# Two products of the next chunk placed ahead of the first output part, and a later load of each chunk's second weight block

## The chip, the core and the metric

The kernel runs on one core of a Trainium2 chip. The metric is the time of one execution on the device in microseconds (us), and the figure for a kernel is the median of several executions. A profiled execution is recorded separately; its trace gives a start and a duration for every instruction of the engines TensorE (PE), VectorE (DVE), ScalarE (ACT) and GpSimd (POOL), and for the transfers that SyncE (SP) issues.

## What is computed

The reference is a two-layer backbone over 512 latent tokens and 256 context tokens of width 1024. Each layer is a SwiGLU half-step, a mixer (a short gated convolution in layer 0, attention in layer 1) and a second SwiGLU half-step. Only the SwiGLU matters here:

```python
def norm_modulate(x, g, shift, scale):
    return rms_norm(x, g) * (1 + scale) + shift

def swiglu(h, w_in, w_out):
    gate, up = jnp.split(h @ w_in, 2, axis=-1)
    return (jax.nn.silu(gate) * up) @ w_out

h = norm_modulate(x_lat, norm_g[i, 0], m_lat[:, 0, 0], m_lat[:, 0, 1])
x_lat = x_lat + MACARON_WEIGHT * m_lat[:, 0, 2] * swiglu(h, ffn_w_in[i, 0], ffn_w_out[i, 0])
```

`w_in` has 2 x 2816 columns and `w_out` 2816 rows. Latent and context tokens share the weights, so a sub-layer works on 768 tokens (512 in the last one).

## The kernel before

**Precision.** Every fp32 weight block is split into a high part (ACT, line 186) and a low part (DVE, line 187), and so is every activation. A product is three matmuls: high by high, high by low, low by high (lines 818 to 820).

**Chunks.** The 2816 columns are 22 chunks of 128 gate and 128 up columns. A chunk c has two raw weight blocks of 512 KB: (c, 0), the gate, and (c, 1), the up columns. Each of the two holds two halves of the contraction, so a chunk has four quarters, `quad(0)` to `quad(3)`. The first few chunks of a sub-layer ("direct" ones: three in the first sub-layer, two in the other SwiGLU ones) are computed by plain products. All later ones use a seven-product scheme over the two halves of the tokens and of the contraction: M1 to M7, with weights that are a quarter or a sum of quarters. M1 and M2 use `quad(0)` and `quad(1)`, which both lie in block (c, 0). M5 is the first that needs block (c, 1): line 354 subtracts a quarter of it, line 363 adds one, and lines 186 and 187 split the result. Below, M1(3) is product M1 of chunk 3.

**Banks of PSUM.** The first sub-layer has three banks A, three C, one B and one S. M1 of a chunk opens a bank A that M6, M7 and M4 go on using; M2 takes the one bank B, which DVE empties at line 1086; M5 opens a bank C for M3. The bank of M1 is copied by ACT at line 1084.

**Output parts.** After chunks 0 and 1 comes output part 0: for each of eight blocks m of `w_out`, a product for the 512 latent tokens and one for the 256 context tokens, each in its own bank. `out_banks` takes the banks C and A in turn. DVE adds each bank, times the gate, to x at line 886. The first three blocks are interleaved, so three banks fill together.

**Order.** PE and SP run in the order in which the code is written; `product_order` gives it, in the first sub-layer with `boot=True`:

- twelve steps of the direct chunks (positions 0 to 11), then M1(3), M2(3), output part 0, M5(3), M6(3),
- then, for each chunk c from 4: M1(c), M2(c), M7(c-1), M5(c), M6(c), M4(c-1), M3(c-1).

ACT and DVE keep the written order up to the second position after the direct steps (13). Behind that a scheduler has fixed their order at build time; it may also put a later instruction in front of an earlier one. At run time each engine works through its own list in order, and a wait holds up all that stands behind it. `hooks` carry other work of the sub-layer by position: the normed activations, their sums T1 to T4, and the splits of these (lines 736 to 778).

**Weights in flight.** Raw blocks go through five buffers (`RAWS`), loaded by SP at line 216 in the order of the list `raws`; a load waits until a buffer is given back, which for the four `w_out` blocks of part 0 (256 KB each) is when both of their splits are done, and for a chunk's two blocks when M3 is prepared. Split weights go through eight buffers (`GRANULES`).

Of the kernel before, what the change touches and what calls it, by code (L numbers as in the profile page):

```python
# [85 lines left out]
def product_order(count, parts, direct, boot=False):  # L86

    ends = {}
    at = 0
    for pi, n in enumerate(parts):
        at += n
        ends[at - 1] = pi
    order = []

    def done(c):  # L100
        if c in ends:
            order.append((ends[c], "out"))

    if boot:
        order += [(c, half + k) for half, k in ("00", "01", "10") for c in range(direct)]
        order += [(c, "11") for c in reversed(range(direct))]
    else:
        order += [(c, h + k) for h in "01" for c in range(2) for k in "01"]
        for c in range(2, direct):
            order += [(c, "10"), (c, "00"), (c, "11"), (c, "01")]  # L110
    order += [(direct, m) for m in ("M1", "M2")]
    for c in range(direct):
        done(c)
    order += [(direct, m) for m in ("M5", "M6")]
    for c in range(direct + 1, count):
        order += [(c, "M1"), (c, "M2"), (c - 1, "M7"), (c, "M5"), (c, "M6"), (c - 1, "M4")]
        if c == count - 1:
            order.append((c, "M7"))
        order.append((c - 1, "M3"))
        done(c - 1)  # L120
    order += [(count - 1, "M4"), (count - 1, "M3")]
    done(count - 1)
    return order
# [3 lines left out]
def backbone(ctx: ExitStack, tc: tile.TileContext, a: dict, out: bass.AP):  # L127
# [23 lines left out]
    def ptile(name, shape=(P, 512)):  # L151
        pool, tag = bank[name]
        return pool.tile(list(shape), F32, name=f"ps_{name}", tag=tag)
# [31 lines left out]
    def split(dsth, dstl, src):  # L185
        act.activation(dsth, src, AF.Copy)  # L186
        dve.tensor_tensor(out=dstl, in0=src, in1=dsth.bitcast(F32), op=ALU.subtract)  # L187
# [6 lines left out]
    raw_tiles = {}  # L194

    def raw_add(src, shape, users):
        raws.append((src, shape, users))
        return len(raws) - 1
# [25 lines left out]
    def raw_used(n):  # L224
        raw_tiles[n][1] -= 1
        if not raw_tiles[n][1]:
            raw_tiles.pop(n)
            if n not in raw_homes:
                raw_state["open"] -= 1
# [64 lines left out]
    def add_plain(raw, u, ks, where=None, event=None):  # L294
        def make(dh, dl):
            split(dh, dl, raw_tiles[raw][0][:, u, ks])
            raw_used(raw)
        stream.append((event, where, ks.stop - ks.start, make))
# [9 lines left out]
    def add_out(w, k0, npart, held=None, key="", events=(None, None), extra=None, event=None):  # L308
        for m in range(0, KC, 2):
            n = raw_add(w[:, m : m + 2, k0 : k0 + npart, :], (2, npart), 2)  # L310
            for u in range(2):
                mm = m + u
                if held and mm // 3 < len(held):
                    add_plain(n, u, slice(0, npart), (key, held[mm // 3], mm % 3), events[mm // 3])
                else:
                    where = extra() if extra else None
                    add_plain(n, u, slice(0, npart), where, event if where else None)

    def add_products(key, sources, order, parts, direct, out_w, held, home=lambda c, kh: None, between=None):

        raw = {}
        seen = set()

        def need(c, which):
            if (c, which) not in raw:
                raw[c, which] = raw_add(sources[c][which], (1, KC), 2 if c < direct else 1)

        for c, which in ((0, 0), (0, 1), (1, 0), (1, 1)):
            need(c, which)
        for c, m in order:  # L330
            if m == "out":
                last = c == len(parts) - 1
                outs = out_w(c)
                add_out(*outs, held=held if last else None, key=f"{key}held", events=((key, "M5"), (key, "M6"), (key, "M3")))
                continue
            for which in range(2):
                need(c, which)
            if (c, m) == (0, "10") and between:
                between()
            if c >= direct:  # L340
                add_product(raw[c, 0], raw[c, 1], m)
            elif (c, m[1]) not in seen:
                seen.add((c, m[1]))
                k0 = 4 * int(m[1])
                for which in range(2):
                    where = home(c, int(m[1]))
                    add_plain(raw[c, which], 0, slice(k0, k0 + 4), where and ("home", (*where, which)))

    def add_product(g, u, m):
        def quad(q):  # L350
            return raw_tiles[g if q < 2 else u][0][:, 0, slice(4 * (q % 2), 4 * (q % 2) + 4)]

        def sub(o, x, y):
            dve.tensor_tensor(out=quad(o), in0=quad(x), in1=quad(y), op=ALU.subtract)  # L354

        def make(dh, dl):
            if m == "M1":
                split(dh, dl, quad(0))
            elif m == "M2":
                split(dh, dl, quad(1))  # L360
            elif m == "M5":
                sub(0, 0, 2)
                dve.tensor_tensor(out=quad(2), in0=quad(2), in1=quad(3), op=ALU.add)
                split(dh, dl, quad(2))
            elif m == "M6":
                sub(2, 3, 0)
                split(dh, dl, quad(2))
            elif m == "M7":
                split(dh, dl, quad(0))
            elif m == "M4":  # L370
                split(dh, dl, quad(3))
            else:
                sub(1, 1, 2)
                split(dh, dl, quad(1))
                raw_used(g)
                raw_used(u)

        stream.append((None, None, 4, make))

    ffn_order = {boot: product_order(FC, FFN_PARTS, BOOT_DIRECT if boot else FFN_DIRECT, boot) for boot in (False, True)}  # L380
    conv_order = product_order(12, (6, 6), CONV_DIRECT)
    conv_pairs = []
    for j in range(0, KC, 2):
# [97 lines left out]
    ada_chunks, ada_loaded, ahead = [], {}, {}  # L481
# [69 lines left out]
    def bg():  # L551

        pace["n"] += 1
        if pace["n"] == pace["first"] - 2:
            for n in range(ahead["depth"]):
                ada_next(ahead["start"] + n)
        bg_run(1)
# [145 lines left out]
    def free_order():  # L703
        region.pop().close()
# [126 lines left out]
            got += [t[:, 0, :], t[:, 1, :]][: count - c]  # L831
        return got

    out_turn = [0]

    def out_banks(grp, count):

        got = []
        for _ in range(count):
            got.append(ptile("CA"[out_turn[0] % 2]))  # L840
            out_turn[0] += 1
        return got

# [169 lines left out]
    def out_phase(*args):  # L1013
        for _ in out_steps(*args):
            pass
# [15 lines left out]
    def products(gp, key, order, parts, direct, chunk, straight, out_args, after, passes, hooks, hold):  # L1031
# [73 lines left out]
        for n, (c, m) in enumerate(order):  # L1105
            if m == "out":
                last = c == len(parts) - 1
                if last and isinstance(after, dict):
                    out_close(*out_args(c), after)
                elif last and after == "end":  # L1110
                    out_last(*out_args(c), gp)
                else:
                    out_phase(geo.groups, passes, *out_args(c), after if last else None, out_banks, 3)
                    if n in hooks:
                        hooks[n]()
                    for go in behind_outs:
                        go()
                    behind_outs.clear()
            elif c < direct:
                directly(n, c, m)  # L1120
            else:
                product(c, m)
                bg()
            if n in hooks and m != "out":
                hooks[n]()
            if n == (steps[-1] + 2 if key == "f00" else steps[-1]):
                free_order()
# [489 lines left out]
    with tc.tile_pool(name="apool", bufs=1) as apool, tc.tile_pool(name="g0", bufs=1) as gp, tc.tile_pool(name="qp", bufs=1) as qp, psum(A=3, B=1, C=3, S=1):  # L1617
# [24 lines left out]
        with tc.tile_pool(name="boot", bufs=1) as bp, aw_pool():  # L1642
# [37 lines left out]
            def do(*items):  # L1680
                def go():
                    for name, *args in items:
                        own[name](*args) if name in own else op[name](*args)
                return go

            def scale_put():
# [19 lines left out]
                     (8, 2): do(("gate1", 1)), (8, 3): do(("gate1", 1)), (9, 0): do(("gate1", 1), ("raws",)), (9, 1): do(("gate1", 1)),  # L1706
                     (10, 0): do(("sum_parted", "T1", 0), ("sum_parted", "T1", 1), ("sums", "T2", 0), ("sums", "T2", 1)),
                     11: do(("fill", 1)), 12: do(("sums", "T3", 0), ("sums", "T3", 1)), 13: do(("sum_parted", "T2", 0), ("sum_parted", "T2", 1)),
                     14: do(("sums", "T4", 0), ("sums", "T4", 1), ("sum_parted", "T3", 0), ("sum_parted", "T3", 1), ("sum_parted", "T4", 0), ("sum_parted", "T4", 1))}
            op1 = opening(0, 1)  # L1710
            ffn(gp, 0, 0, op1, TOKENS, hooks, op)
        op2 = opening(0, 2)
# [91 lines left out]
```

## Time and profile before

| | us |
|---|---|
| median of three runs | 2451.38 |
| lowest and highest of the runs | 2450.44, 2451.80 |
| profiled execution, its own time | 2457.93 |
| span of the profiled execution (first to last instruction) | 2456.2 |
| PE busy in it | 2402.6 |
| DVE busy | 2019.5 |
| ACT busy | 1167.3 |
| mean granted PE clock | 0.993 |

The busy time of an engine says how much of the span it had work on it. PE's is nearly all of the span, so the places of interest are the few in which PE stood still, and what it waited for there. A timeline row gives start, duration, engine, line, what is written and read, the shape, how many instructions are merged, and in brackets the idle time ahead of it with what ended that. Rows overlap a little: a row's duration includes its pipeline, and the next one may start before it is over.

### The profile page before, as it was taken

The page shows a single profiled execution, that of the slowest core. Times are in us where ns is not written, and L with a number is a line of the kernel's source. Part 1 is how long each engine was busy: PE and PEld are TensorE (multiplying, and loading weights), DVE is VectorE, ACT ScalarE, POOL GpSimd, SP SyncE. Part 2 cuts the span into 40 slices and gives each one's busy share as a digit, 9 for nine tenths or more (in the row PEclk, how much of TensorE's full clock was granted, in tenths as well). Part 3 has the DMA queues.
Part 4 walks back from the last instruction along what each step waited for, and adds up shares of the span by engine and source line. Part 5 has one row for each costly group of instructions (what it writes and reads, how often), then busy time and mean ns, then how long its engine had stood idle before and what let it go on. Part 6 is the DMA issues. An engine that isn't in the chain of part 4 may idle for free.

```text
span 2456.2 us, 37712 instructions
## 1 busy us (share of the span) xinstructions
PE 2402.6 (98%) x14303; PEld 2268.6 (92%) x14303; DVE 2019.5 (82%) x4011; ACT 1167.3 (48%) x2205; POOL 134.6 (5%) x256
## 2 busy tenths in 40 slices
PE   8999999999999999999999999999999999999998
PEld 5799999999999999999999999999997889899997
DVE  5889999678988889897667999976568887887776
ACT  5544343355535643433435544344346776555545
POOL 0001111000000001110000012200000000000000
PEclk9999999999999999999999999999999999999999
DMA  8234453230333024433222146542231101133332
GB/s 310 86 121 131 144 163 121 78 121 26 95 108 126 23 75 142 159 120 104 86 66 69 51 140 209 176 130 63 68 120 53 51 1 48 57 108 101 102 104 78
DMA packets 93062, 253.71 MB, mean 103 GB/s; under 512 B 10320, under 2 KB 18640, under 8 KB 92880
## 3 DMA queue, kind: packets, MB, share of 16 engines
q1 hardware_dynamic: 71984, 183.65, 23.3%
q0 software_dynamic: 20352, 67.12, 9.2%
q8 instruction: 112, 1.84, 0.3%
q14 instruction: 70, 0.57, 0.1%
q10 hardware_dynamic: 544, 0.52, 0.1%
HBM read 249.16 MB, written 2.10 MB: 102 GB/s over the span
## 4 chain that ended last, share of the span: by engine, by line
PE 65%; issue 20%; DVE 9%; ACT 3%; DMA 3%; POOL 0%; SPq 0%; DVEq 0%; ACTq 0%; POOLq 0%
PE ps_A L818 11%; PE ps_A L819 11%; PE ps_A L820 11%; PE ps_C L818 7%; PE ps_C L819 7%; PE ps_C L820 7%; PE ps_B L818 2%; PE ps_B L819 2%; PE ps_B L820 2%; DVE w L187 2%; DVE ps_S L511 1%; DMA aw<-in_ada_t 1%; PE ps_T L1474 1%; DMA raw<-in_ffn_w_in 1%; DMA silu_row<-in_crow 1%
## 5 line engine op out<-in xcount | busy, mean ns | idle before, releaser
L186 ACT ACTIVATE w<-raw 128x512 fp32r<-128x512 f32 (+1 forms) x868 | 525.0, 619 | 705.7 <-PE ps_A L820 339.3
L187 DVE TENSOR_TENSOR w<-raw,w 128x512 fp32r<-128x512 f32 (+1 forms) x868 | 578.8, 679 | 109.1 <-ACT w L186 99.8
L818 PE MATMUL ps_C<-gh,w 128*128 128x512 f32 (+1 forms) x544 | 195.2, 359 | 12.2 <-DVE g L1100 9.1
L819 PE MATMUL ps_C<-gl,w 128*128 128x512 f32 (+1 forms) x544 | 194.1, 357 | 0.0
L820 PE MATMUL ps_C<-gh,w 128*128 128x512 f32 (+1 forms) x544 | 193.6, 356 | 0.0
L354 DVE TENSOR_TENSOR raw<-raw,raw 128x512 f32<-128x512 f32 x264 | 181.3, 689 | 12.5 <-DMA raw<-in_ffn_w_in 9.1
L489 POOL DMA_DIRECT2D aw<-in_ada_t x240 | 129.0, 538 | 1060.6 <-DVE mods L511 603.0
L818 PE MATMUL ps_A<-gh,w 128*128 128x256 f32 (+1 forms) x544 | 181.0, 333 | 3.0 <-DVE x L886 3.0
L820 PE MATMUL ps_A<-gh,w 128*128 128x256 f32 (+1 forms) x544 | 181.0, 333 | 0.0
L819 PE MATMUL ps_A<-gl,w 128*128 128x256 f32 (+1 forms) x544 | 181.0, 333 | 0.0
L511 DVE CUSTOM_DVE_ANT_0 ps_S<-aw,silu_row,mods 128x512 f32<-128x512 f32 x208 | 157.5, 757 | 11.1 <-ACT silu_row L495 9.3
L511 DVE CUSTOM_DVE_ANT_0 ps_S<-aw,silu_row,packed 128x512 f32<-128x512 f32 x208 | 157.2, 756 | 6.3 <-DMA aw<-in_ada_t 4.7
L886 DVE SCALAR_TENSOR_TENSOR x<-ps_C,gat,x 128x512 f32<-128x512 f32 (+1 forms) x156 | 102.8, 659 | 68.3 <-PE ps_C L820 68.3
L886 DVE SCALAR_TENSOR_TENSOR x<-ps_A,gat,x 128x512 f32<-128x512 f32 (+1 forms) x164 | 100.3, 611 | 41.3 <-PE ps_A L820 41.1
L818 PE MATMUL ps_A<-tB11h,w 128*128 128x384 f32 (+1 forms) x400 | 130.7, 327 | 0.2 <-ACT tB11h L758 0.2
L818 PEld LDWEIGHTS ps_C<-gh,w 128*128 128x128 f32 x544 | 103.3, 190 | 29.6 <-issue 9.1
L819 PE MATMUL ps_A<-tB11l,w 128*128 128x384 f32 (+1 forms) x400 | 130.4, 326 | 0.2 <-DVE tB11l L759 0.2
L820 PE MATMUL ps_A<-tB11h,w 128*128 128x384 f32 (+1 forms) x400 | 130.4, 326 | 0.0
L819 PE MATMUL ps_C<-tB22l,w 128*128 128x384 f32 (+2 forms) x384 | 125.2, 326 | 0.0
L820 PE MATMUL ps_C<-tB22h,w 128*128 128x384 f32 (+2 forms) x384 | 124.7, 325 | 0.0
L818 PE MATMUL ps_C<-tB22h,w 128*128 128x384 f32 (+2 forms) x384 | 124.6, 325 | 0.0
L820 PEld LDWEIGHTS ps_C<-gh,w 128*128 128x128 f32 x544 | 103.4, 190 | 15.1
(437 smaller groups left out, 6942.9 us busy)
## 6 DMA issues: line engine op xcount, KB each, us to landing
raw<-in_ffn_w_in SPq DMA_DIRECT2D x170, 512.0 KB, 4.1
aw<-in_ada_t POOLq DMA_DIRECT2D x240, 256.0 KB, 3.1
raw<-in_ffn_w_out SPq DMA_DIRECT2D x80, 512.0 KB, 4.4
raw<-in_conv_w_in SPq DMA_DIRECT2D x24, 512.0 KB, 3.7
ada<-in_ada_w SPq DMA_DIRECT2D x28, 256.0 KB, 5.3
raw<-in_attn_w_qkv SPq DMA_DIRECT2D x12, 512.0 KB, 5.0
raw<-in_ada_w SPq DMA_DIRECT2D x8, 512.0 KB, 6.7
silu_row<-in_crow POOLq DMA_DIRECT2D x8, 512.0 KB, 4.2
```

The source lines that it names most:

```text
L186: act.activation(dsth, src, AF.Copy)
L187: dve.tensor_tensor(out=dstl, in0=src, in1=dsth.bitcast(F32), op=ALU.subtract)
L354: dve.tensor_tensor(out=quad(o), in0=quad(x), in1=quad(y), op=ALU.subtract)
L489: nc.gpsimd.dma_start(w, a["ada_t"][t, kh, j])
L511: ins = dve.tensor_tensor_reduce(out=junk, in0=w, in1=silu_row[kh][:, v, :], scale=1.0, scalar=total if kh else ada_b[:, i, hm // 2, col : ...
L818: pe.matmul(ps, wh, xh, start=first, stop=False, **kw)
L819: pe.matmul(ps, wh, xl, start=False, stop=False, **kw)
L820: pe.matmul(ps, wl, xh, start=False, stop=last, **kw)
L886: dve.scalar_tensor_tensor(out=x, in0=p[:, o - off : o - off + w], scalar=gat[:, m, v : v + 1], in1=x, op0=ALU.mult, op1=ALU.add)
L1474: pe.transpose(pt[:, c, :], pr[:, (c0 + c) * P : (c0 + c + 1) * P], ident)
```

## The change

- In the first sub-layer alone (`ahead = 2`), M1(4) and M2(4) stand in front of output part 0, behind M2(3). From M7(3) on the order is what it was.
- In every sub-layer, M1 and M2 of a chunk ask for the first raw block alone; the second one is asked for at M5. This changes the order of the loads where output part 0 stands between M2 and M5: the four `w_out` blocks are then loaded ahead of the second block. That is so in all four SwiGLU sub-layers; in the first one the block (4, 0) moves ahead too.
- In the first sub-layer's part 0 the banks are taken in the turn C, B, C, A, C instead of C, A; M1(3) and M1(4) hold two of the three banks A meanwhile.
- The hook at position 14 is at 16, which is the same place behind output part 0.

```diff
-    order += [(direct, m) for m in ("M1", "M2")]
+    ahead = 2 if boot else 1
+    order += [(direct + c, m) for c in range(ahead) for m in ("M1", "M2")]
     for c in range(direct):
         done(c)
     order += [(direct, m) for m in ("M5", "M6")]
     for c in range(direct + 1, count):
-        order += [(c, "M1"), (c, "M2"), (c - 1, "M7"), (c, "M5"), (c, "M6"), (c - 1, "M4")]
+        if c >= direct + ahead:
+            order += [(c, "M1"), (c, "M2")]
+        order += [(c - 1, "M7"), (c, "M5"), (c, "M6"), (c - 1, "M4")]
...
-            for which in range(2):
+            for which in range(1 if m in ("M1", "M2") else 2):
                 need(c, which)
...
-    out_turn = [0]
+    out_turn, out_tags = [0], ["CA"]
...
-            got.append(ptile("CA"[out_turn[0] % 2]))
+            got.append(ptile(out_tags[0][out_turn[0] % len(out_tags[0])]))
...
+                    out_tags[0] = "CBCAC" if key == "f00" and c == 0 else "CA"
                     out_phase(geo.groups, passes, *out_args(c), after if last else None, out_banks, 3)
+                    out_tags[0] = "CA"
...
-                     14: do(("sums", "T4", 0), ...
+                     16: do(("sums", "T4", 0), ...
```

`add_product` gets the table of raw blocks instead of two of its numbers, so that the second block's number need not be known at M1.

More of the change, by code (lines that the diff above doesn't have):

```diff
@@ L340, in add_products @@
             if c >= direct:
-                add_product(raw[c, 0], raw[c, 1], m)
+                add_product(raw, c, m)
             elif (c, m[1]) not in seen:
@@ L347, in add_products, with add_product @@
                     add_plain(raw[c, which], 0, slice(k0, k0 + 4), where and ("home", (*where, which)))
-    def add_product(g, u, m):
+    def add_product(raw, c, m):
         def quad(q):
-            return raw_tiles[g if q < 2 else u][0][:, 0, slice(4 * (q % 2), 4 * (q % 2) + 4)]
+            return raw_tiles[raw[c, q // 2]][0][:, 0, slice(4 * (q % 2), 4 * (q % 2) + 4)]
         def sub(o, x, y):
@@ L374, in make @@
                 split(dh, dl, quad(1))
-                raw_used(g)
-                raw_used(u)
+                raw_used(raw[c, 0])
+                raw_used(raw[c, 1])
         stream.append((None, None, 4, make))
@@ L1708, in backbone @@
                      11: do(("fill", 1)), 12: do(("sums", "T3", 0), ("sums", "T3", 1)), 13: do(("sum_parted", "T2", 0), ("sum_parted", "T2", 1)),
-                     14: do(("sums", "T4", 0), ("sums", "T4", 1), ("sum_parted", "T3", 0), ("sum_parted", "T3", 1), ("sum_parted", "T4", 0), ("sum_parted", "T4", 1))}
+                     16: do(("sums", "T4", 0), ("sums", "T4", 1), ("sum_parted", "T3", 0), ("sum_parted", "T3", 1), ("sum_parted", "T4", 0), ("sum_parted", "T4", 1))}
             op1 = opening(0, 1)
```

## The prediction

> **What bounds the kernel now.** I read the busy times first, then the list of what PE waited for, and then the timelines of PE and DVE around output part 0 of the first sub-layer, where the change sits.
>
> ```profile
> PE 2402.6 (98%) x14303; PEld 2268.6 (92%) x14303; DVE 2019.5 (82%) x4011; ACT 1167.3 (48%) x2205; POOL 134.6 (5%) x256
> ```
>
> PE is busy for 98% of the span, so an edit that leaves PE's own work alone can only win back time in which PE stands still or runs on a slow clock. The list of PE's waits names two of the longest, and the timeline of PE puts both in output part 0:
>
> ```profile
> PE ps_A L818 <- DVE x L886: 3.7, 2, 3.0
> PE ps_C L818 <- ACT w L186: 2.8, 1, 2.8
> ...
> 93.47 0.34 PE L820 MATMUL ps_B<-tB21h,w 128*128 128x384 f32 x1
> 96.57 0.50 PE L818 MATMUL ps_C<-gh,w 128*128 128x512 f32 x1 [2.77 <-ACT w L186]
> 105.52 0.58 PE L818 MATMUL ps_A<-gh,w 128*128 128x256 f32 x1 [2.98 <-DVE x L886]
> 118.34 0.34 PE L818 MATMUL ps_C<-tT1h,w 128*128 128x384 f32 x1
> 122.50 0.33 PE L818 MATMUL ps_A<-tB11h,w 128*128 128x384 f32 x1
> 126.71 0.34 PE L818 MATMUL ps_A<-tT3h,w 128*128 128x384 f32 x1
> ```
>
> M2(3) ends near 93.8. PE waits 2.77 for the first split of an output weight, starts part 0 at 96.57, and stops again for 2.98 because DVE has not yet emptied a bank. M5(3) and M6(3) run from 118.34 to 122.50 (4.16 for both), M1(4) and M2(4) from 122.50 to 126.71 (4.21), where M7(3) begins. The clock by stretches, PE alone (length, PE busy with its count, granted clock, and two columns on DMA):
>
> ```profile
> 95.29:98.71 3.42, 2.14 (x9) 1.00 0.07 7
> ...
> 102.12:105.53 3.41, 0.43 (x5) 1.00 0.72 249
> 105.53:108.94 3.41, 3.41 (x11) 0.50 0.01 4
> 2139.87:2143.28 3.41, 1.41 (x13) 1.00 0.74 209
> 2143.28:2146.69 3.41, 3.41 (x19) 0.50 0.24 99
> ```
>
> After the second wait the clock is at half for 3.41 us, which costs half of that, 1.71. It fell just so after a stretch with 2.00 us idle (3.41 less 1.41).
>
> How long part 0 takes without a wait is shown by the same part in the third sub-layer, which has the same shapes:
>
> ```profile
> 857.54 0.39 PE L818 MATMUL ps_C<-gh,w 128*128 128x512 f32 x1
> 863.08 0.28 PE L818 MATMUL ps_A<-gh,w 128*128 128x256 f32 x1
> 874.24 0.34 PE L818 MATMUL ps_C<-tT1h,w 128*128 128x384 f32 x1
> ```
>
> That is 16.70 us. So from 93.8 to 126.71, 32.9 us, PE's work is 16.70 + 4.16 + 4.21 = 25.1, and 7.8 is lost: 2.77 and 2.98 of waiting, 1.71 by the half clock, and some 0.4 of slower restarts. 7.8 is 0.32% of the time, and all that the change can win here.
>
> **The first wait: does it go?** PE would now find M1(4) at 93.8 in place of part 0. What it needs is a split weight, and ACT has none ready:
>
> ```profile
> 95.69 0.52 ACT L1184 ACTIVATE gh<-gd 128x384 fp32r<-128x384 f32 x1 [0.71 <-DVE gd L1205]
> 96.12 1.94 ACT L186 ACTIVATE w<-raw 128x256 fp32r<-128x256 f32 x6
> 119.38 0.62 ACT L186 ACTIVATE w<-raw 128x512 fp32r<-128x512 f32 x1
> ```
>
> The six splits of output weights begin at 96.12, behind the last step of the direct chunks (line 1184). In the changed kernel's instruction order the two splits for M1(4) and M2(4) stand at that same place, behind line 1184 and ahead of the output weights. Could line 1184 come earlier? The change takes two operations off DVE before it:
>
> ```profile
> 80.08 0.69 DVE L354 TENSOR_TENSOR raw<-raw,raw 128x512 f32<-128x512 f32 x1
> 80.81 0.69 DVE L363 TENSOR_TENSOR raw<-raw 128x512 f32<-128x512 f32 x1
> 80.88 0.62 ACT L1173 ACTIVATE gd<-gd,bias 128x384 f32<-128x384 f32 x1 [3.40 <-DVE bias L1171]
> 81.69 0.62 DVE L1175 SCALAR_TENSOR_TENSOR gd<-gd,bias 128x384 f32<-128x384 f32 x1
> ```
>
> These are the subtraction and addition for M5(3). But the next step, line 1175, needs ACT's line 1173, which ends at 81.50. So the two hide behind that wait, their removal gains nothing, and the chain up to 96.12 stays. A split of 512 columns takes 0.62, so M1(4) starts at about 96.8: the wait is 3.0, not 2.77. The first wait stays, 0.2 longer.
>
> **The second wait: what takes its place.** I lay DVE's new list end to end from the time at which its last direct step is done, with these durations (starts of neighbours are 0.08 closer than the durations, as 96.72 against 96.25 + 0.56 shows):
>
> ```profile
> 96.25 0.56 DVE L1186 TENSOR_TENSOR gl<-gd,gh 128x384 fp32r<-128x384 f32 x1 [0.59 <-ACT gh L1184]
> 96.72 2.09 DVE L187 TENSOR_TENSOR w<-raw,w 128x256 fp32r<-128x256 f32 x6
> 98.73 1.82 DVE L778 TENSOR_TENSOR fT<-f,f 128x768 f32<-128x768 f32 x2
> 101.53 0.55 DVE L1086 TENSOR_TENSOR g<-ps_B,g 128x384 f32<-128x384 f32 x1
> 102.33 1.82 DVE L187 TENSOR_TENSOR tT2l<-f,tT2h 128x768 fp32r<-128x768 f32 x2
> 104.06 0.74 DVE L886 SCALAR_TENSOR_TENSOR x<-ps_C,gat,x 128x512 f32<-128x512 f32 x1
> 111.52 0.95 DVE L187 TENSOR_TENSOR tT3l<-fT,tT3h 128x768 fp32r<-128x768 f32 x1
> 112.38 1.29 DVE L187 TENSOR_TENSOR w<-raw,w 128x512 fp32r<-128x512 f32 x2
> ```
>
> The changed list reads: two splits of 512 columns (96.8 to 98.0), four of 256 (0.335 each, to 99.35), the two sums fT (1.74, to 101.1), one more split (to 101.4), and only then line 1086, which empties bank B of M2(3), to 101.95. There is one bank B, and M2(4) needs it. M1(4) takes half of 4.21, 2.1, and has to wait a little for its low part (97.4), so it ends at 99.3. PE then stands still until 102.0: 2.7 us, in place of the 2.98.
>
> M2(4) takes 2.1 and, by the restarts above, some 0.25 more: part 0 begins at 104.35. With 16.70 for it and 4.16 for M5(3) and M6(3), M7(3) would begin at 125.2, against 126.71: 1.5 sooner, if the clock stays up. If it is at half for 3.41 us after the new wait, it is 126.9, 0.2 later.
>
> Does DVE keep up then? Behind M2(4) it has, before its first eviction: line 1086 for chunk 4 (0.47, at 104.5 at the earliest), two subtractions and an addition of 0.60 each for M5(3) and M5(4), one split (0.335) and a tT3l (0.87). That ends at 108.0, and the eviction at 108.75. PE needs that bank C back for the third 256-wide bank, which by the rows of the third sub-layer is 5.54 (863.08 less 857.54) after the start of part 0, at 109.9. The cover is 1.1 us thin, but it holds. Bank B for the second block of part 0 is free at about 105.0, when PE has done the three matmuls before it.
>
> **The later load.** In the third sub-layer SP issues the last output weights at 856.2, as the first of them give their buffer back; now the second block goes at that point (the fourth sub-layer has the same shapes):
>
> ```profile
> 791.46 65.13 SPq L216 DMA_DIRECT2D raw<-in_ffn_w_out  x4
> ...
> DMA to landing us min/median/max: 2.7/4.1/10.6
> ```
>
> With the median landing it is there at 860.3 and even with the longest at 866.8. Two operations of 0.69 and two splits of 0.62 and 0.69 later it can be used, at 863 to 869.5, and M5 begins at 874.24. That is hidden by part 0. In the last sub-layer part 0 is shorter:
>
> ```profile
> 2117.43 0.37 SPq L216 DMA_DIRECT2D raw<-in_ffn_w_out  x1
> 2128.66 0.28 PE L818 MATMUL ps_C<-tT1h,w 128*128 128x256 f32 x1
> ```
>
> The block goes out at 2117.8, lands at 2121.9, and M5 needs it 6.8 us later, with 2.6 of work between. I take nothing for it; the longest landing (2128.4) would make M5 late by 2.3.
>
> **The sum.** Against the profiled execution (2457.93; span 2456.2): 0.2 more for the first wait, 0.3 less for the second, nothing for the restarts, and half a clock in place of half a clock: 0.2 later at 126.7 by the laid-out chain. The runs' median, 2451.38, is 6.55 below the profiled execution; I carry the difference over, to 2451.6.
>
> The clock is where I had to choose. Both new waits (3.0 and 2.7) are longer than the 2.00 that sufficed at 2143.28, so I take one half-clock stretch that costs 1.71, as in the trace; the one after the first wait would fall on M1(4), whose slowness the second wait hides. The Trainium skill, "TensorE: Matmul & The Clock Gate", section "Why this matters for your kernels", says that PE idle gaps above about 3 us are to be avoided, because one idle window of the clock gate (some 3.4 us, by "What's actually happening") halves the clock. By that rule neither new wait would lower it, and the sum would be 2449.9. The trace disagrees: 2.00 us idle in a stretch of 3.41 was enough. The same page says that the window runs free of the kernel, so that it falls differently in each execution; no run here shows that yet.
>
> **The rivals.**
> - *The clock stays up* after the second wait: 2449.9. For it: the first wait, 2.77, left the clock at full, since it was spread over two stretches (the one to 98.71 had 1.28 of it). Chance 0.22.
> - *A second half-clock stretch* counts as well, since two waits stand within 8 us: 1.7 more, 2453.3. Against it: the second wait hides it. Chance 0.08.
> - *The moved products cover DVE's backlog*: 4.2 us of matmuls stand where PE waited, and part 0 starts that much later, so both waits and the half clock go: 7.8 less, 2443.8. Against it: M1(4) needs the split behind line 1184, and M2(4) needs bank B. Chance 0.08.
> - *Slower: the blocks (3, 1) and (4, 1) land too late, and DVE's evictions stand behind them.* The subtraction for M5(4) now precedes the first eviction in DVE's list, and it waits for block (4, 1), which cannot be issued before the last split out of an output weight block, at 102.3. Landing by 107.7 harms nothing (0.60 + 0.87 + 0.74 later is 109.9). That is 5.4 us after the issue, the median is 4.1. With the longest, 10.6, PE stands still for 5.2 and pays 1.71 for the clock: 2458.5. Chance 0.09.
> - *The second block is late in the last sub-layer*, and a half clock follows: by 2.3 + 1.7, 2455.6; with DVE's evictions behind it, more. Chance 0.03.
>
> **How the numbers follow.** The forecast has 0.50. About 0.2%, 4.9 us, is what a measurement of this kernel can tell from no change. Within it lie the forecast and the two clock cases: 0.80. Faster is the cover rival, 0.08. Slower is late landing, 0.09, and the last sub-layer, 0.03 (it is near the bound, and more when evictions queue): 0.12. The range of 2449.0 to 2455.0 holds the forecast and the clock cases with some 0.9 for the uncertain restarts below and 1.7 above, and leaves out the other 0.20.
>
> **What would show it.** Right: a PE wait of about 3.0 for ACT's split ahead of M1(4), and one of about 2.7 ahead of M2(4) that ends with DVE's line 1086; none for line 886 in part 0; M7(3) begins between 125 and 127. Wrong: if M2(4) starts with no wait, DVE's chain is not what holds it; if PE waits for line 886 near 110, the late block decides; and if the waits in part 0 are gone but the time isn't lower, the loss has moved behind M7(3), where DVE must still empty M7(3)'s bank in time for M4(3).

## The result, and the profile after

| | kernel before | changed kernel |
|---|---|---|
| median of 10 runs each on one chip, us | 2451.64 | 2458.52 |
| lowest and highest | 2450.44, 2454.57 | 2456.24, 2460.80 |
| ratio to before, 95% interval | | 1.0022 [1.0014, 1.0030] |
| profiled execution, us | 2457.93 | 2456.74 |

The change makes the kernel 0.22% slower, 5.4 us by the ratio, where I had forecast no change (2451.6). (The two medians lie 6.9 us apart; the ratio is the estimate that comes with an interval, so sizes go by it.) The two profiled executions say the opposite, 1.2 us less, and that is a first lesson: a single execution of this kernel can be off the median by more than the whole effect (before's profiled one is 6.3 above this median; on the chips of the experiments below, the same kernel's medians were 2453.65 to 2455.46). So sizes are read from the runs below, and mechanisms from the traces.

The busy times of the page after: PE has the same work as before.

```profile
PE 2402.9 (98%) x14303; PEld 2268.2 (92%) x14303; DVE 2020.6 (82%) x4011; ACT 1168.9 (48%) x2205; POOL 134.6 (5%) x256
```

PE's waits of the changed kernel between 60 and 140 us. There were two around output part 0, of 2.8 and 3.0; now there are three. (Helper lines are 3 higher than before: 821 is the old 818, 889 the old 886, 1089 the old 1086, 1095 the old 1092.)

```profile
PE ps_A L821 <- ACT w L189: 2.8, 1, 2.8
PE ps_A L821 <- ACT g L1095: 1.8, 1, 1.8
PE ps_B L821 <- ACT tT2h L189: 1.4, 1, 1.4
```

The timeline of PE shows where they stand: ahead of M1(4) (96.43), of M2(4) (101.73), and of M7(3) (127.00). Part 0 begins at 103.92, M5(3) at 120.89, and the last matmul of M6(3) at 124.88.

```profile
93.32 0.34 PE L823 MATMUL ps_B<-tB21h,w 128*128 128x384 f32 x1
96.43 0.45 PE L821 MATMUL ps_A<-tB11h,w 128*128 128x384 f32 x1 [2.77 <-ACT w L189]
101.73 0.42 PE L821 MATMUL ps_B<-tB21h,w 128*128 128x384 f32 x1 [1.41 <-ACT tT2h L189]
103.92 0.39 PE L821 MATMUL ps_C<-gh,w 128*128 128x512 f32 x1
120.89 0.34 PE L821 MATMUL ps_C<-tT1h,w 128*128 128x384 f32 x1
124.88 0.34 PE L823 MATMUL ps_A<-tT2h,w 128*128 128x384 f32 x1
127.00 0.45 PE L821 MATMUL ps_A<-tT3h,w 128*128 128x384 f32 x1 [1.77 <-ACT g L1095]
```

The granted clock by stretches (columns: length, PE busy with its count, clock, DMA share and GB/s). Two stretches of the changed kernel are at half clock: one right after the first wait, one right after the new wait ahead of M7(3).

```profile
94.22:97.64 3.42, 1.10 (x5) 1.00 0.00 0
97.64:101.05 3.41, 2.69 (x9) 0.50 0.46 151
124.95:128.36 3.41, 1.64 (x10) 1.00 0.57 197
128.36:131.77 3.41, 3.41 (x12) 0.50 0.31 115
```

What does M7(3) wait for? M6 and M7 of a chunk write the same bank A: ACT has to copy M6(3)'s result out of it (line 1095) before M7(3) may write. The timeline of ACT in the changed kernel has that copy behind three weight splits, which themselves stood still until DVE had made a difference of raw quarters (line 357):

```profile
124.90 1.67 ACT L189 ACTIVATE w<-raw 128x512 fp32r<-128x512 f32 x3 [0.52 <-DVE raw L357]
126.48 0.47 ACT L1095 ACTIVATE g<-ps_A 128x384 f32<-128x384 f32 x1
```

In the timeline of ACT in the kernel before, the same copy (line 1092) waited for PE alone:

```profile
122.70 0.49 ACT L1092 ACTIVATE g<-ps_A 128x384 f32<-128x384 f32 x1 [2.70 <-PE ps_A L820]
```

There it was over at 123.19, and PE had M1(4) and M2(4) to do until 126.71. The change moved just these two products away, so M7(3) stands right behind M6(3). M6(3) ends at 125.22 in the changed kernel (124.88 + 0.34), and the copy begins 1.26 later. The three splits ahead of it are for M3(3), M1(5) and M2(5), which come four to six products after M7(3); that order of ACT was fixed at build time.

### The profile page after: what moved, and what is told of

It reads as the page before. It is cut to its first block, busy times and chain, and to the rows that moved or that the text cites. A ratio compares the mean times of both kernels' runs of the same rounds, so it can differ in the third digit from the quotient of the medians.

```text
span 2455.0 us, 37710 instructions
## 1 busy us (share of the span) xinstructions
PE 2402.9 (98%) x14303; PEld 2268.2 (92%) x14303; DVE 2020.6 (82%) x4011; ACT 1168.9 (48%) x2205; POOL 134.6 (5%) x256
## 4 chain that ended last, share of the span: by engine, by line
PE 64%; issue 18%; DVE 10%; ACT 4%; DMA 3%; POOL 0%; SPq 0%; DVEq 0%; ACTq 0%; POOLq 0%
PE ps_A L822 11%; PE ps_A L821 11%; PE ps_A L823 11%; PE ps_C L821 7%; PE ps_C L822 7%; PE ps_C L823 7%; DVE w L190 2%; PE ps_B L823 2%; PE ps_B L821 2%; PE ps_B L822 2%; DVE ps_S L514 1%; DMA silu_row<-in_crow 1%; DMA ada<-in_ada_w 1%; ACT f L752 1%; PE ps_T L1479 1%
## 5 line engine op out<-in xcount | busy, mean ns | idle before, releaser
L823 PE MATMUL ps_A<-gh,w 128*128 128x256 f32 (+1 forms) x534 | 177.7, 333 | 0.0
L821 PE MATMUL ps_A<-gh,w 128*128 128x256 f32 (+1 forms) x534 | 177.6, 332 | 0.0
L889 DVE SCALAR_TENSOR_TENSOR x<-ps_A,gat,x 128x256 f32<-128x256 f32 (+1 forms) x159 | 97.7, 614 | 40.9 <-PE ps_A L823 40.7
```

The source lines that it names most:

```text
L821: pe.matmul(ps, wh, xh, start=first, stop=False, **kw)
L823: pe.matmul(ps, wl, xh, start=False, stop=last, **kw)
L889: dve.scalar_tensor_tensor(out=x, in0=p[:, o - off : o - off + w], scalar=gat[:, m, v : v + 1], in1=x, op0=ALU.mult, op1=ALU.add)
```

## The experiments

Each group of four kernels ran on one chip beside the kernel before, 11 or 12 runs a kernel and 33 to 35 of the one before (medians 2454.40, 2453.65 and 2455.46 in the three groups). Kernels of different groups are compared by their ratios. A ratio's interval is about 0.09% (2.2 us) to either side, so a difference of two ratios is known to some 3 us, and the waits carry the finer argument.

| kernel | median, us | ratio to before | 95% interval | PE's waits around part 0, us |
|---|---|---|---|---|
| e1, changed kernel again | 2460.12 | 1.0021 | 1.0012 to 1.0030 | 2.8, 1.1, 1.8 |
| e2, late load alone | 2454.58 | 0.9997 | 0.9988 to 1.0006 | 2.5, 2.2 |
| e3, cover put back | 2457.09 | 1.0006 | 0.9998 to 1.0015 | 2.8, 1.2 |
| e4, late load in first sub-layer alone | 2459.94 | 1.0021 | 1.0012 to 1.0030 | 2.8, 1.4, 1.8 |
| e5, before without the cover | 2454.74 | 1.0001 | 0.9992 to 1.0010 | 2.8, 1.1, 0.6 |
| e6, e3 and early split | 2457.10 | 1.0012 | 1.0003 to 1.0021 | 6.0, 0.5 |
| e7, e3 and bank C | 2451.82 | 0.9994 | 0.9985 to 1.0003 | 2.8 |
| e8, e3 with both | 2450.78 | 0.9989 | 0.9980 to 0.9998 | 1.3, 1.3 |
| e9, copy ahead of two splits | 2457.75 | 1.0009 | 1.0001 to 1.0018 | 2.8, 1.1, 0.7 |
| e13, changed kernel and bank C | 2455.44 | 0.9998 | 0.9990 to 1.0007 | 2.8, 0.6 |
| e10, e8 with later sums | 2452.75 | 0.9985 | 0.9977 to 0.9994 | 1.4, 0.2 |
| e11, before with later sums | 2453.66 | 0.9989 | 0.9980 to 0.9997 | 3.0, 0.6 |

**e1, the changed kernel unaltered**, on the chip of the next three.

> The changed kernel, unaltered, timed on one chip together with the kernel before. Its trace shows it ended 1.2 us sooner than the trace of before (span 2455.0 against 2456.2), while its ten runs have a median 6.9 us above those of before. Theory 'cover': M1(4) and M2(4) stood between M6(3) and M7(3) and gave ACT time to copy bank A (line 1092 of before); now M7(3) waits 1.8 us for that copy and a half-clock stretch follows (1.7 us): 1.8 to 3.5 us slower than before. Rival 'late load': the second block, loaded later in the last three SwiGLU sub-layers, costs the rest: some 7 us slower. Rival 'execution': the two traces are right and the difference of the medians comes from chips or executions: within 2 us of before.

The loss came again on another chip, with the same wait of 1.77 ahead of M7(3) and a half-clock stretch behind it, from 128.07 on.

**e2, the late load alone.** The kernel before, with one part of the change:

```diff
-            for which in range(2):
+            for which in range(1 if m in ("M1", "M2") else 2):
                 need(c, which)
```

> The order of before, with only the second raw block of a chunk asked for at M5, in all SwiGLU sub-layers. 'Late load': most of the loss stays, 4 us or more over before. 'Cover' and 'execution': within 1.5 us of before.

0.9997: the later load costs nothing that can be measured. Its trace shows something else: with the order of the kernel before, the two waits are

```profile
PE ps_C L818 <- ACT w L186: 2.5, 1, 2.5
PE ps_A L818 <- DVE x L886: 2.2, 1, 2.2
```

In its timeline they are 2.55 and 2.24, together 1.0 less than in the profiled execution on which the prediction stands (2.77 and 2.98).

**e3, the cover put back.** The changed kernel, with M5(4) between M6(3) and M7(3) in the first sub-layer:

```diff
-        order += [(c - 1, "M7"), (c, "M5"), (c, "M6"), (c - 1, "M4")]
+        order += [(c, "M5"), (c - 1, "M7"), (c, "M6"), (c - 1, "M4")] if boot and c == direct + 1 else [...]
```

> The changed kernel with M5(4) moved from behind M7(3) to between M6(3) and M7(3), in the first sub-layer. M5(4) takes 2.1 us of PE in a bank C of its own. 'Cover': the wait of 1.8 us ahead of M7(3) is gone, and with it the half clock behind it: 1.8 to 3.5 us faster than the changed kernel. 'Late load' and 'execution': within 1 us of the changed kernel.

The waits of e3 have no line 1095 left, and the ratio falls from 1.0021 to 1.0006, 3.7 us:

```profile
PE ps_A L821 <- ACT w L189: 2.8, 1, 2.8
PE ps_B L821 <- DVE g L1089: 1.2, 1, 1.2
```

No half-clock stretch stands behind M7(3) in its trace either. So the wait ahead of M7(3), with the half clock behind it, is by these ratios the larger part of the loss, though 3.7 us are known to some 3 us only. What is left above the kernel before is within the interval.

**e4, the late load in the first sub-layer alone.** The changed kernel, with `range(1 if key == "f00" and m in ("M1", "M2") else 2)`.

> The changed kernel with the second block asked for at M5 in the first sub-layer only; the three other SwiGLU sub-layers load as before. 'Late load': some 4 us or more faster than the changed kernel. 'Cover' and 'execution': within 1 us of the changed kernel.

1.0021, as for the changed kernel: the later loads of the other sub-layers are no part of the loss.

**e5, the cover taken out of the kernel before.** M7(3) ahead of M1(4) and M2(4), nothing else:

```diff
-        order += [(c, "M1"), (c, "M2"), (c - 1, "M7"), (c, "M5"), (c, "M6"), (c - 1, "M4")]
+        order += [(c - 1, "M7"), (c, "M1"), (c, "M2"), (c, "M5"), (c, "M6"), (c - 1, "M4")] if boot and c == direct + 1 else [...]
```

> The kernel before, with one thing changed in the first sub-layer: M7(3) stands right behind M6(3), ahead of M1(4) and M2(4); output part 0, the loads and the banks are as before. Theory (cover): M6(3) and M7(3) share one bank A, and M7(3) must wait until ACT has copied M6(3)'s result; M1(4) and M2(4) covered that. Then PE waits 1.8 us for ACT's copy ahead of M7(3), and a half-clock stretch of 1.7 us may follow: 1.8 to 3.5 us slower than the kernel before, with the two waits around part 0 (2.8 and 3.0) kept. Rival (the loss of the change is made by the products ahead of part 0: their waits, or DVE's list): no wait ahead of M7(3), and the time of the kernel before within 1 us.

My theory missed here. The wait is there, but it is 0.6 and not 1.8, and the time does not move (1.0001):

```profile
PE ps_C L818 <- ACT w L186: 2.8, 1, 2.8
PE ps_A L818 <- DVE x L886: 1.1, 1, 1.1
...
PE ps_A L818 <- ACT g L1092: 0.6, 1, 0.6
```

In e5 ACT stands idle when M6(3) ends and copies at once. 0.6 is what the missing cover itself costs; the other 1.2 of the changed kernel must be ACT's list. e9 tests that.

**e6, the split for M1(4) earlier.** e3, with `(11, 0): do(("fill", 1))` added to the hooks, so that this split stands ahead of ACT's last step of the direct chunks (line 1189).

> The kernel of e3_cover, with one more thing: the split of M1(4)'s weight is written one step earlier, so that on ACT it stands ahead of the last step of the direct chunks (line 1189). Theory (the wait ahead of M1(4) is ACT's order): that wait, 2.8 us in e3_cover, goes, and M1(4) begins right behind M2(3). The time comes down by 2.8 us at most, and by less if M2(4) then stands longer for bank B (its wait 1.2 becomes up to 4.0, and nothing is gained). Rival (M1(4) waits for something else, its block or DVE): the wait stays at 2 us or more, and the time is that of e3_cover within 1 us.

The wait ahead of M1(4) is gone, and M2(4) waits all the longer. From the timeline of PE in e6:

```profile
101.60 0.66 PE L821 MATMUL ps_B<-tB21h,w 128*128 128x384 f32 x1 [5.96 <-ACT tT2h L189]
```

M2(4) begins at 101.60, within 0.13 of the changed kernel's 101.73, whether M1(4) is early or not. Bank B sets this time, through DVE's list: line 1089, which empties it, ends 0.15 earlier in e6 (101.45) and 0.14 earlier in the changed kernel (101.59). The label names the last of several semaphores. In e6 the two waits are merged into one of 6.0, a whole stretch of the clock without a matmul, and two stretches follow one another at half clock:

```profile
97.95:101.36 3.41, 0.00 (x0) 0.50 0.58 187
101.36:104.78 3.42, 3.18 (x10) 0.50 0.59 188
```

So nothing was gained, as the expectation had for this case; the ratio is no better than e3's.

**e7, M2(4) in a bank C.** e3, with two lines ahead of the bank's allocation:

```diff
+            if key == "f00" and c == direct + 1 and m == "M2":
+                tag = "C"
```

> The kernel of e3_cover, with one more thing: M2(4) takes a bank C in place of bank B. Theory (M2(4)'s wait of 1.2 is for DVE to empty bank B): it goes, and the time comes down by 1 to 3 us against e3_cover, by whether a half-clock stretch goes with it. Rival (M2(4) would wait for its own split weight as well): the wait stays at 1 us or more with another name, and the time is that of e3_cover within 1 us.

One wait is left, and the ratio falls by 0.12% against e3, 2.9 us for 1.2 us of waiting (the excess is within the uncertainty; the two traces differ by 1.2 there, as the table further below shows):

```profile
PE ps_A L821 <- ACT w L189: 2.8, 1, 2.8
```

**e8, both edits on e3.**

> The kernel of e3_cover with both edits: the split of M1(4)'s weight one step earlier, and M2(4) in a bank C. If both waits go and nothing replaces them, 4.0 us of waiting and 1.7 us of half clock are won against e3_cover: 4 to 6 us less, which is 1.5 to 3.5 us less than the kernel before. If DVE is then late with its evictions in output part 0, PE waits there for line 889, and the time is that of e3_cover within 1 us.

4.2 us below e3 by the ratios, 2.7 below the kernel before, and the first version whose interval lies under 1. The size is the expected one, but the waits did not both go: 2.5 us of them are left, and what went as well is the half clock, of which this trace has none around part 0. Bank B is late here too, now for the second block of part 0 (the second line):

```profile
PE ps_C L821 <- ACT w L189: 1.3, 1, 1.3
PE ps_B L821 <- ACT tT2h L189: 1.3, 1, 1.3
```

**e9, ACT's copy ahead of two of the three splits.** The changed kernel, in which no weight behind M4(3)'s (the expectation writes M4(4)) is split before M7(3) asks for its own:

```diff
-            if where is None and state["open"] >= GRANULES:
+            if where is None and state["open"] >= GRANULES or n >= 30 and state["used"] < 26:
```

> The changed kernel, with one more thing: no weight behind M4(4)'s is split before M7(3) asks for its own, so that in ACT's list the copy of M6(3)'s bank (line 1095) stands ahead of two of the three splits that stood before it; the split for M3(3) still does. Theory (the wait ahead of M7(3) is 0.6 of the copy itself, which nothing covers, and the rest is ACT's list): that wait is 0.7 to 0.9 us in place of 1.8, and the time is 1.0 to 2.7 us below the changed kernel (1.0 of waiting, and up to 1.7 if the half-clock stretch behind it goes in most executions). Rival (the wait is a price of putting M7(3) right behind M6(3), whatever ACT's list): it stays at 1.5 or more and the time is that of the changed kernel within 1 us.

The timeline of ACT in e9: one split ahead of the copy, and the others behind it.

```profile
125.41 0.63 ACT L189 ACTIVATE w<-raw 128x512 fp32r<-128x512 f32 x1 [0.52 <-DVE raw L357]
125.94 0.47 ACT L1095 ACTIVATE g<-ps_A 128x384 f32<-128x384 f32 x1
126.31 1.14 ACT L189 ACTIVATE w<-raw 128x512 fp32r<-128x512 f32 x2
```

Its wait list has 0.7 for line 1095 in place of 1.8:

```profile
PE ps_B L821 <- DVE g L1089: 1.1, 1, 1.1
PE ps_A L821 <- ACT g L1095: 0.7, 1, 0.7
```

The ratio is 0.13% lower than the changed kernel's, 3.2 us. That is a little over the 1.0 to 2.7 expected, within its uncertainty. No half-clock stretch follows M7(3) in this trace.

**e13, the changed kernel with M2(4) in a bank C**, the two lines of e7. The scheduler then also places the copy (line 1097 here) ahead of all three splits.

> The changed kernel, with M2(4) in a bank C in place of bank B; M7(3) stays right behind M6(3). At build time this also moves ACT's copy of M6(3)'s bank ahead of all three splits that stood before it. Theory: the wait of M2(4) (1.4 us) goes, and the one of M7(3) comes down to the copy's own 0.6; the time is 3 to 6 us below the changed kernel, so 0 to 1 us from the kernel before or under it. Rival (only M5(4) between M6(3) and M7(3) takes the wait away): M7(3) still waits 1.5 or more, and the time is 1.4 to 3 us below the changed kernel.

```profile
PE ps_A L821 <- ACT w L189: 2.8, 1, 2.8
PE ps_A L821 <- ACT g L1097: 0.6, 1, 0.6
```

The copy in the timeline of ACT in e13, with nothing but M6(3) to wait for:

```profile
123.89 0.49 ACT L1097 ACTIVATE g<-ps_A 128x384 f32<-128x384 f32 x1 [1.50 <-PE ps_A L823]
```

The wait of M2(4) is gone, that of M7(3) is the 0.6 of e5, and the ratio is 0.9998, 5.9 us below the changed kernel. So the order of the change, with M7(3) right behind M6(3), isn't slow in itself: bank B and ACT's list made it so.

**e10 and e11, the sums for T3 later.** In e8 and in the kernel before, the two sums (1.8 us of DVE) move from the hook at 12 to the one behind part 0.

> The kernel of e8_both, with the two sums for T3 (1.8 us of VectorE, line 781) written behind output part 0 in place of the slot ahead of it. The build-time order then puts other sums earlier, into VectorE's gaps between the last direct steps, and line 1091, which empties bank B, comes right behind the weight splits. Theory (VectorE's list holds bank B): the wait of part 0's second block, 1.25 us in e8_both, goes, and the time is 1 to 3 us below e8_both. Rival (the sums in the gaps delay the last direct steps, and with them the split that M2(4) waits for): that wait, 1.25, grows by 0.5 to 1.5, and the time is that of e8_both or up to 2 us above.

> The kernel before, with the two sums for T3 (1.8 us of VectorE, line 778) written behind output part 0 in place of the slot ahead of it; nothing else. Theory (the second wait in the kernel before, 2.98 us for line 886, is VectorE's list): it comes down to 1.2 or less, and the time is 1 to 3.5 us below the kernel before. Rival: the sums go into gaps that are none, the first wait grows by 0.5 to 1.5 and the time is within 1 us of the kernel before.

The waits of e10, and below them those of e11:

```profile
PE ps_C L821 <- ACT w L189: 1.4, 1, 1.4
...
PE ps_C L823 <- DVE w L190: 0.2, 1, 0.2
```

```profile
PE ps_C L818 <- ACT w L186: 3.0, 1, 3.0
PE ps_A L818 <- DVE x L886: 0.6, 1, 0.6
```

In e10 the wait for bank B is gone; at 0.9985, 3.7 us under the kernel before, it has the lowest ratio, though it can't be told from e8 (0.9989), and its median is 2.7 under. In e11 the second wait of the kernel before falls from 2.98 to 0.6, and this one edit is worth 0.11%, 2.7 us, as expected. The first waits grew by about 0.2 in both, so the rival has a little in it.

## Why the prediction was wrong, point by point

**The part that held.** The loss around part 0 of the kernel before was put at 7.8 us, in two waits and a half clock; that a part of it could be won by other means than the change is shown by e10 (3.7 won by the ratio). The wait ahead of M1(4) stayed, 2.77 where I had 3.0, and M1(4) began at 96.43 (96.8). DVE's new list ran as I had laid it out. From the timeline of DVE in the changed kernel, the row that ends M2(4)'s wait and the first eviction of part 0:

```profile
101.03 0.56 DVE L1089 TENSOR_TENSOR g<-ps_B,g 128x384 f32<-128x384 f32 x1
...
107.60 0.75 DVE L889 SCALAR_TENSOR_TENSOR x<-ps_C,gat,x 128x512 f32<-128x512 f32 x1
```

Bank B is empty at 101.59 (forecast 101.95), M2(4) begins at 101.73 (102.0), part 0 at 103.92 (104.35), the first eviction ends at 108.35 (108.75), none is waited for, and M6(3) ends at 125.22, where I had put the start of M7(3) with a warm clock at 125.2. Block (4, 1) came in time, so the rival that ends slower through late landing did not happen; that its 2458.5 is the measured median is chance. Nor did the one in the last sub-layer (e4).

**The step that failed** is the sentence "With 16.70 for it and 4.16 for M5(3) and M6(3), M7(3) would begin at 125.2". It sets M7(3) end to end behind M6(3) and gives that joint no price, though I had quoted the rows which show M1(4) and M2(4) between the two in the kernel before. I costed the moved products at the place they went to and not at the place they left, where 4.21 us of PE covered a copy of the bank that M6(3) and M7(3) share. It measured 1.77 in place of nothing, of which 0.6 is the copy (e5, e13) and 1.2 is ACT's list, three splits not needed yet and the DVE difference they wait for (e9 takes 1.0 of it away, e13 all). A small slip stands beside it: the terms of the sum, 0.2 more and 0.3 less, make 0.1 less, while the laid-out chain has 0.2 more; the forecast took the chain.

**The clock** cost in the trace what I had put down for it, but for another reason. I had one stretch at half clock that costs 1.71, behind the second new wait. The first new wait did lower the clock, and that stretch was hidden by the wait for bank B, as forecast (1.41 left of 2.7). Behind the second new wait the clock stayed up. The stretch that costs, 3.41 us at half clock, fell behind M7(3), where nothing waits that could hide it, and the wait that I had at nothing stands right ahead of it. That 1.71 is the forecast size is luck, and so is M7(3)'s start at 127.00, the edge of the "between 125 and 127" that was to show me right: I had reached 126.9 with the half clock, and the trace got there with 1.77 of waiting instead and had the half clock still to come. Over all runs, the mean clock and span of each give (1 - clock) x span as the time lost to the clock: 14.1 us in the 33 runs of the kernel before, 16.3 in the 11 of e1. So some 2.2 of the 5.2 us between their means are clock. The split is rough: each run's clock is recorded in steps of 0.001 (2.5 us), and a stretch that a wait hides counts too.

**How much of the loss the traces show.** PE does the same matmuls in the same order in all these kernels but for the 446th to the 613th. So the time from its 431st (near 91) to its 701st (near 146 in the kernel before) can be compared in every trace, and so can all the rest of the span:

| kernel | 431st to 701st matmul, us | rest of the span, us |
|---|---|---|
| before | 55.1 | 2401.1 |
| e2, the order of before | 54.2 | 2398.8 |
| e5, the same without the cover | 53.9 | 2395.8 |
| e11, before with later sums | 53.2 | 2399.7 |
| changed kernel | 57.2 | 2397.8 |
| e1, the same | 57.2 | 2401.1 |
| e4, late load in first sub-layer alone | 55.6 | 2398.6 |
| e9, copy ahead of two splits | 54.6 | 2400.1 |
| e3, cover put back | 53.6 | 2401.7 |
| e13, changed kernel and bank C | 52.7 | 2401.7 |
| e7, e3 and bank C | 52.4 | 2399.2 |
| e6, e3 and early split | 55.5 | 2395.3 |
| e8, e3 with both | 50.8 | 2398.2 |
| e10, e8 with later sums | 49.6 | 2400.6 |

Around part 0 the change costs 2.1 us in the pair of traces on which I had worked, and up to 3.0 against e2. Without the half clock behind M7(3), in e4, it costs 0.5 to 1.4. The edits that shorten or remove M7(3)'s wait win 2.6 (e9), 3.6 (e3) and 4.5 (e13, which has no wait of M2(4) either) against e1, which bears out the order of the ratios. The rest of the span, where PE does the same, varies by 6.4 us from trace to trace; the changed kernel's was 3.3 shorter than that of before, and e1's was not. This is why the two profiled executions said the opposite of the medians.

**The base.** The profiled execution of before was one of its longer ones, 2457.93, and its two waits (5.75) were longer than in other executions of the same order (4.8 in e2, and 3.9 in e5 without the 0.6 ahead of M7(3)). In e5 the granted clock shows half speed right behind the first wait, so that DVE caught up while PE was slow:

```profile
93.03:96.44 3.41, 0.65 (x5) 1.00 0.00 0
96.44:99.85 3.41, 3.41 (x8) 0.50 0.43 124
```

I subtracted the waits of this one execution and carried the whole difference to the median over as a constant. So up to 3 of the 5.4 us are found in the traces, with their cause; the rest is in none of them, is about as large as the uncertainty of the ratio, and stays open.

**The chances.** None of the five rivals decided, and what did was not among them. "If the waits in part 0 are gone but the time isn't lower, the loss has moved behind M7(3)" named the place within one product, but for DVE's emptying of M7(3)'s bank in time for M4(3), not for ACT's copy of M6(3)'s result.

## What to carry to other kernels

When an instruction is moved, price the place it leaves as well: list what ran beside it there, above all the copy of a bank between two products that accumulate into the same one, and look where that copy stands in the copying engine's list. A wait on TensorE can cost twice its length through the clock that follows: 1.77 and 1.71 more in two of the three traces that have it. And where the effect sought is 0.2%, take the size of a stall from several executions of the old kernel, not from one trace of it.

## What the runs showed of the hardware

**The clock's stretches run free of the kernel.** In the trace of before, two half-clock stretches begin at 105.53 and 2143.28: 2037.75 apart, which is 597 times 3.4133. In the changed kernel they begin at 97.64 and 128.36, 9 times 3.413 apart. So they lie on one grid. The grid lies differently in each execution: 105.53 and 97.64, each counted from its own first instruction, are 2.3 stretches apart, no whole number. The Trainium skill, "TensorE: Matmul & The Clock Gate", section "What's actually happening", says that the window is 3413 ns and free-running, and the traces agree. The grid is a likely reason, among others, why equal kernels differ by several us from run to run (2450.8 to 2458.7 for the one before in the first group): the time lost to the clock and the span rise together there, with a correlation of 0.82, and of 0.56 and 0.48 in the other two groups.

**About half a stretch of idle time can be enough.** The wait of 1.77 ahead of M7(3) was at half clock afterwards in the changed kernel, after a stretch in which PE was busy for 1.64. In e4 the same wait of 1.77 was not, after one with 1.70. The granted clock in e4:

```profile
123.82:127.24 3.42, 1.70 (x10) 1.00 0.28 87
127.24:130.65 3.41, 3.37 (x19) 1.00 0.64 220
```

The rule of the Trainium skill, "TensorE: Matmul & The Clock Gate", section "Why this matters for your kernels", against gaps above about 3 us would have let this wait pass; the measured 1.64 decides against it. The border isn't sharp in PE's busy time. In the trace of before, a stretch with 1.49 was not followed by half clock, and one with 1.85 was:

```profile
668.73:672.15 3.42, 1.49 (x8) 1.00 0.19 75
672.15:675.56 3.41, 3.41 (x15) 1.00 0.09 11
2075.02:2078.43 3.41, 1.85 (x14) 1.00 0.00 0
2078.43:2081.84 3.41, 3.41 (x19) 0.50 0.00 0
```

A wait near 1.7 us is therefore a throw of the dice, and one of 0.6 or 0.7 (e13, e9) left the clock up.
